# Expert weights of a routed SwGLU layer: 32 KB per partition in five joined slots from the third expert on, instead of 16 KB in ten

## The chip, the cores and the metric

The kernel runs on one core of a Trainium2 chip (trn2), as one program with one launch. Time is device time in microseconds (us), from the first to the last instruction of an execution with what lies around it; a run's time is one execution, and medians are over several. All numbers are float32.

## What is computed

One layer of a diffusion backbone: 512 latent tokens and 256 context tokens of width 1024. The first sub-layer (a state-space branch and a latent-attention branch, gated and merged) is not touched by the change. The second is a set of 16 experts, each of which picks its 64 best tokens. Cut to what matters:

```python
def expert_choice_ffn(h, w_router, w_gate, w_up, w_down):
    aff = jax.nn.softmax((h @ w_router).astype(jnp.float32), axis=-1)
    gate, idx = lax.top_k(aff.transpose(0, 2, 1), cap)              # cap = 64 of 512 tokens
    xs = h[bidx, idx]
    hid = jax.nn.silu(jnp.einsum('becd,edf->becf', xs, w_gate)) * jnp.einsum('becd,edf->becf', xs, w_up)
    ys = jnp.einsum('becf,efd->becd', hid, w_down) * gate[..., None].astype(h.dtype)
    return jnp.zeros_like(h).at[bidx, idx].add(ys)
```

The weights of one expert are gate and up, 1024 x 2816 each, and down, 2816 x 1024: 33 MiB in float32, 528 MiB for the 16. Every one of them is used once.

## The kernel before

The first sub-layer, the router and the top-64 selection come first. Then the experts run one after the other, in a Python loop that is unrolled (`for e in range(NE)`, L1487). An expert's hidden width of 2816 is cut into six chunks: five of 512 columns and one of 256. Each chunk goes through two steps.

- `hidden` (L1501 to 1515; called H below): for 8 slices of the input width, one matmul with the gate weights and one with the up weights (L1505, tile `pgu`), then SiLU on ScalarE (L1507, tile `hd`), the product on VectorE (L94), four transposes on TensorE (L1512, `phT`) and a copy back to SBUF on ScalarE (L1514, `hT`).
- `down` (L1517 to 1521; called D): two matmuls for each 128 hidden columns, added up over the expert in one PSUM tile (L1520, `pdn`).

After the last chunk one VectorE instruction weights the result (`ye`), and GpSimd adds its rows into the output by an indirect DMA (L1539). `gather(e + 1)`, which builds the next expert's input (`pxg`, `pxt`, `pinf` on TensorE), is written ahead of chunk 3. A scheduler sets the order on each engine; on SyncE's queue (SP), which issues all weight loads, it is the order of the code.

The weights are stored in blocks that are ready for the loads: `w_e_gu` has 11 blocks of 128 x 4096 for an expert (two for each chunk of 512, holding the first and the second four slices of the input width; one for the last chunk), `w_e_down` has 5 blocks of 128 x 4096, and `w_e_down_end` one of 128 x 2048. So an expert has 16 loads of 2 MiB, with 16 KB for each partition, and one of 1 MiB. `ring` (L1442) puts each 2 MiB load into the next of ten slots in the fixed order `RING`; the slots are pools of one buffer each, and a load waits until the readers of the slot's last contents are done. At most eight loads are under way at a time: each has one of eight completion semaphores in turn, and SP waits for the load that had it last. The ten slots lie where the first sub-layer's tiles lay, so the first loads are issued as that memory comes free.

The last expert is written with each D behind the next chunk's H. All others are written H, D, H, D.

Of the kernel before, what the change touches and what calls it, by code (L numbers as in the profile page):

```python
# [18 lines left out]
D = 1024  # L19
# [7 lines left out]
NE = 16  # L27
# [21 lines left out]
NPK = _off  # L49
NTRI = 193  # L50
NR, NL = 13, 7

RING = ("L0", "R1", "R3", "R5", "R2", "R4", "R0", "L1", "L2", "L3")

# [2 lines left out]
def hybrid_block(ctx: ExitStack, tc: tile.TileContext, A, out, dbg=None, stop=99):  # L57
    nc = tc.nc
    V, S, G, T = nc.vector, nc.scalar, nc.gpsimd, nc.tensor
    dma, dmr = nc.sync.dma_start, G.dma_start  # L60

    def pool(name, st=ctx, **kw):
        return st.enter_context(tc.tile_pool(name=name, bufs=kw.pop("bufs", 1), reuse_waits="tile", **kw))
# [6 lines left out]
    cur = {}  # L70
# [13 lines left out]
    def pg(name, shape=(128, 512)):  # L84
        return psg.tile(list(shape), F32, name=name, tag="pg")
# [94 lines left out]
    rows = {}  # L180
# [35 lines left out]
    for j in range(4):  # L216
        t = tl("xx", f"X{j}", [NCH, 2, D])
# [416 lines left out]
    for k in range(8):  # L634
# [4 lines left out]
        h = tl("gt", "hxf", [128, 512])  # L639
# [222 lines left out]
    for gb in range(4):  # L862
# [16 lines left out]
        t, y = s5_T(gb, yb)  # L879
# [85 lines left out]
    t = tl("gt", "krt2", [128, 6, 32])  # L965
# [346 lines left out]
    for b in range(8):  # L1312
        if b % 4 == 0:
            wmo = wload("w_mla_o", 0, 4, 128 * b, 512)
        if b % 2 == 0:
            c = 256 * ((b % 4) // 2)
            wms = wsplit(wmo[:, :, c:c + 256], 4, 256)
        c = 128 * (b % 2)
# [11 lines left out]
    for n in range(2):  # L1330
        for kh in range(2):
            w = wload("w_out", 4 * kh, 4, 512 * n, 512)
# [101 lines left out]
    chunks = [(512 * i, 512) for i in range(5)] + [(2560, 256)]  # L1434
    nring = [0]
    ph2.close()
    for n in ("R0", "R1", "R2", "R3", "R4", "R5", "small"):
        cur[n] = pool(n, side="right")
    for n in ("L0", "L1", "L2", "L3"):
        cur[n] = pool(n)  # L1440

    def ring(name, src, rn):  # L1442

        w = src.shape[1]
        r = "small"
        if w > 2048:
            r = RING[nring[0] % len(RING)]
            nring[0] += 1
        t = tl(r, name, [128, w])
        dma(t, src)  # L1450
        return [t[:, w // rn * i:w // rn * (i + 1)] for i in range(rn)]

    def gather(e):

# [31 lines left out]
    nxt_ = gather(0)  # L1486
    for e in range(NE):  # L1487
        xe, ge, sidx = nxt_
        wgu, wd, wds = [A[n][e] for n in ("w_e_gu", "w_e_down", "w_e_down_end")]
        po = pg("pdn")  # L1490

        def load_gu(f0, fn):
            if fn == 256:
                return ring("wgu", wgu[10], 16)
            a, b = [ring("wgu", wgu[f0 // 256 + i], 8) for i in range(2)]
            return a[:4] + b[:4] + a[4:] + b[4:]

        def load_d(f0, fn):
            return ring("wd", wds, 2) if fn == 256 else ring("wd", wd[f0 // 512], 4)

        def hidden(wt_, fn):  # L1501
            p = pw("pgu", (128, 512))
            for k in range(8):
                for j in range(2):
                    T.matmul(p[64 * j:64 * j + 64, :fn], xe[:, k, :], wt_[8 * j + k], start=(k == 0), stop=(k == 7))  # L1505
            hd = l2("hd", [64, 512])
            S.activation(hd[:, :fn], p[0:64, :fn], AF.Silu)  # L1507
            mul(hd[:, :fn], hd[:, :fn], p[64:128, :fn])
            ph = pa("phT", (128, 4, 64))
            n = fn // 128  # L1510
            for b in range(n):
                T.transpose(ph[:, b, :], hd[:, 128 * b:128 * b + 128], ident[0:64, 0:64])  # L1512
            hT = l2("hT", [128, 4, 64])
            S.copy(hT[:, :n], ph[:, :n])  # L1514
            return hT

        def down(hT, td, f0):  # L1517
            for b, w in enumerate(td):
                for h in range(2):
                    T.matmul(po[64 * h:64 * h + 64, :], hT[:, b, :], w[:, 512 * h:512 * h + 512],  # L1520
                             start=(f0 == 0 and b == 0), stop=(f0 + 128 * b == FF - 128))

        if e < NE - 1:
            for f0, fn in chunks:
                if f0 == 1536:
                    nxt_ = gather(e + 1)
                wt_, td = load_gu(f0, fn), load_d(f0, fn)
                down(hidden(wt_, fn), td, f0)
        else:
            hts = []  # L1530
            for i, (f0, fn) in enumerate(chunks):
                hts.append(hidden(load_gu(f0, fn), fn))
                if i:
                    f1, fm = chunks[i - 1]
                    down(hts[i - 1], load_d(f1, fm), f1)
            down(hts[-1], load_d(f0, fn), f0)
        ye = l2("ye", [128, 512])
        stt(ye, po, ge, g2bc, ALU.mult, ALU.mult)
        G.indirect_dma_start(out=o2, out_offset=bass.IndirectOffsetOnAxis(ap=sidx, axis=0),  # L1539
                             in_=ye, in_offset=None, compute_op=ALU.add)  # L1540
# [3 lines left out]
def layout(inputs):  # L1544
    import numpy as np

    a = {k: np.asarray(v) for k, v in inputs.items()}
    f32 = np.float32
    pk = np.zeros((128, NPK), f32)

    def put(n, v):
        o, w = PK[n]
        pk[:v.shape[0], o:o + w] = v

    def cols(v):
        return np.ascontiguousarray(v.reshape(-1, 128).T)

    def ssm(v):
        rest = v.shape[3:]
        v = v.reshape((2, 4, 2, 4, 64) + rest)  # L1560
        v = np.moveaxis(v, (2, 4, 1, 0, 3), (0, 1, 2, 3, 4))
        return np.ascontiguousarray(v).reshape((128, 32) + rest)

    put("c", cols(a["c"][0]))
    put("cc", cols(a["c_ctx"]))
    put("bada", cols(a["b_ada"][0]))
    put("g1n", cols(a["norm1_g"][0]))
    put("g2n", cols(a["norm2_g"][0]))
    put("qag", cols(a["q_a_g"][0]))
    put("kvag", cols(a["kv_a_g"][0]))  # L1570
    put("bglu", cols(a["b_glu"][0]))
    put("sd", a["ssm_d"][0].reshape(4, 2, 4, 16).transpose(2, 1, 3, 0).reshape(128, 4))
    put("lre", ssm(a["ssm_lam_re"][0]))
    put("lim", ssm(a["ssm_lam_im"][0]))
    put("ldt", ssm(np.broadcast_to(a["ssm_log_dt"][0][:, :, None], (2, 32, 64))))
    put("gq", a["q_norm_g"][0][:, None])
    put("gk", a["k_norm_g"][0][:, None])
    sw = np.arange(32).reshape(2, 2, 8)[:, ::-1].reshape(-1)
    gq, gk = a["q_norm_g"][0][64:], a["k_norm_g"][0][64:]
    put("grope", np.broadcast_to(np.concatenate([gq, gq[sw], gk, gk[sw]]), (128, 128)))  # L1580
    tok = (8 * np.arange(64)[None, None, :] + 2 * np.arange(4)[:, None, None] + np.arange(2)[None, :, None]).reshape(4, 128)
    inv = f32(10000.0) ** (-np.arange(8, dtype=f32) / f32(8))
    pos = np.stack([tok // 64, tok % 64], -1).astype(f32)
    ang = (pos[..., None] * inv).astype(np.float64)
    cs, sn = np.cos(ang), np.sin(ang)
    cs = np.stack([cs, cs], 3).reshape(4, 128, 32)
    sn = np.stack([-sn, sn], 3).reshape(4, 128, 32)
    put("rcos", cs.transpose(1, 0, 2).reshape(128, 128).astype(f32))
    put("rsin", sn.transpose(1, 0, 2).reshape(128, 128).astype(f32))
    put("tok", tok.T.astype(f32))  # L1590
    put("ident", np.eye(128, dtype=f32))
    put("hmask", np.tile(np.eye(16, dtype=f32), (8, 1)))
    put("stack", np.tile(np.eye(32, dtype=f32), (4, 1)))

    def ct(v):
        return ssm(np.swapaxes(v, -1, -2))

    tri = np.zeros((128, NTRI), f32)
    tri[:, :128] = np.triu(np.ones((128, 128), f32))
    tri[:, 128:192] = np.arange(1, 65)  # L1600
    tri[64:, 192] = 1
    r = {"pk": pk, "tri": tri,
         "ssm_b": np.ascontiguousarray(np.stack([ssm(a["ssm_b_re"][0]), ssm(a["ssm_b_im"][0])], 1)),
         "ssm_c": np.ascontiguousarray(np.stack([ct(a["ssm_c_re"][0]), ct(a["ssm_c_im"][0])], 1)),
         "x": a["x"][0], "ctx": a["ctx"][0]}
    for n in ("w_ada", "b_ada", "w_in", "w_qb", "w_kvb", "w_mla_o", "w_glu", "w_ssm_o", "w_out", "w_router"):
        r[n] = a[n][0]

    w = [a[n][0].reshape(NE, 8, 128, FF).transpose(0, 2, 1, 3) for n in ("w_e_gate", "w_e_up")]
    b = np.empty((NE, 11, 128, 2, 2048), f32)  # L1610
    for i in range(2):
        m = w[i][..., :2560].reshape(NE, 128, 2, 4, 5, 512).transpose(0, 4, 2, 1, 3, 5)
        b[:, :10, :, i] = m.reshape(NE, 10, 128, 2048)
        b[:, 10, :, i] = w[i][..., 2560:].reshape(NE, 128, 2048)
    r["w_e_gu"] = b.reshape(NE, 11, 128, 4096)
    w = a["w_e_down"][0]
    r["w_e_down"] = w[:, :2560].reshape(NE, 5, 4, 128, D).transpose(0, 1, 3, 2, 4).reshape(NE, 5, 128, 4096)
    r["w_e_down_end"] = w[:, 2560:].reshape(NE, 2, 128, D).transpose(0, 2, 1, 3).reshape(NE, 128, 2048)
    return {k: np.ascontiguousarray(v) for k, v in r.items()}


# [17 lines left out]
```

## Time and profile before

| What | us |
| --- | --- |
| median of 3 runs | 1923.01 (1919.36 to 1924.98) |
| the profiled execution | 1919.85 |
| its span, from first to last instruction | 1918.1 |
| TensorE busy with matmuls in it | 1633.8 (85%) |
| VectorE / ScalarE / GpSimd busy in it | 531.5 / 320.7 / 209.9 |

The span falls into two stretches. In the first 620 us, the first sub-layer, the engines share the work and the DMA engines are partly idle. From there to the end TensorE and the DMA engines are both nearly always at work, and the other engines rest. Busy TensorE time is the time in which some matmul was under way, and says nothing of how well it was used.

### The profile page before, as it was taken

To read this page: it belongs to the slowest core of one execution; us is meant where nothing else is said; L and a number is where in the kernel's file an instruction comes from. 1 tells how busy PE (TensorE), PEld (TensorE's weight loads), DVE (VectorE), ACT (ScalarE), POOL (GpSimd) and SP (SyncE) were. 2 spreads that over 40 slices of the span, in tenths; PEclk is the share of its full clock that TensorE was granted. 3 is DMA by queue.
4 is the path that set the end of the run, shared out by engine and by line. 5 is a ranking of instruction groups with operands and counts; after the bars stand their busy time and mean duration, and the time that the engine had idled before them with its cause. 6 is when DMAs were issued, how large, how long until landed. Compare 5 with 4: busy or idle time off the path is not lost.

```text
span 1918.1 us, 20921 instructions
## 1 busy us (share of the span) xinstructions
PE 1633.8 (85%) x8660; PEld 791.5 (41%) x8660; DVE 531.5 (28%) x1180; ACT 320.7 (17%) x593; POOL 209.9 (11%) x218
## 2 busy tenths in 40 slices
PE   3798999999995988888888888888888788888886
PEld 2586778755573333333333333323223232332322
DVE  7877665675745101011000100001000010100000
ACT  3422225364421000000000000000000000000000
POOL 3667200231110000000000000000000000000000
PEclk8899999999997999999999999999999999999999
DMA  9243353525539899999999999999999999999996
GB/s 316 57 141 111 105 189 133 170 97 201 157 90 401 363 422 426 422 427 420 422 427 422 421 426 422 426 423 423 425 421 427 421 427 421 420 428 421 427 422 281
DMA packets 108654, 642.56 MB, mean 335 GB/s; under 512 B 10256, under 2 KB 45072, under 8 KB 73232
## 3 DMA queue, kind: packets, MB, share of 16 engines
q1 hardware_dynamic: 105040, 631.79, 81.2%
q0 software_dynamic: 2880, 7.34, 1.7%
q10 hardware_dynamic: 640, 2.10, 0.3%
q8 instruction: 68, 1.11, 0.2%
q14 instruction: 26, 0.21, 0.0%
HBM read 623.93 MB, written 17.27 MB: 334 GB/s over the span
## 4 chain that ended last, share of the span: by engine, by line
PE 43%; DMA 36%; DVE 8%; issue 5%; ACT 3%; POOL 2%; POOLq 0%; ACTq 0%; SPq 0%; DVEq 0%
DMA wgu<-in_w_e_gu 18%; PE pgu L1505 14%; DMA wd<-in_w_e_down 10%; PE pdn L1520 8%; DMA wd<-in_w_e_down_end 6%; PE pxg L1462 2%; PE po L1263 1%; DVE hd L94 1%; PE px L122 1%; PE px L124 1%; PE px L123 1%; ACT hd L1507 1%; PE ada L191 1%; PE phT L1512 1%; PE py L801 1%
## 5 line engine op out<-in xcount | busy, mean ns | idle before, releaser
L1505 PE MATMUL pgu<-wgu,xe 128*64 128x512 f32 (+1 forms) x3072 | 644.9, 559 | 27.5 <-DMA wgu<-in_w_e_gu 26.0
L1505 PEld LDWEIGHTS pgu<-wgu,xe 128*64 128x64 f32 x3072 | 219.9, 137 | 426.5 <-issue 351.1
L1520 PE MATMUL pdn<-wd,hT 128*64 128x512 f32 x1408 | 357.5, 645 | 34.5 <-ACT hT L1514 34.5
L94 DVE TENSOR_TENSOR hd<-hd,pgu 64x512 f32<-64x512 f32 x96 | 61.9, 645 | 994.3 <-ACT hd L1507 994.3
L1507 ACT ACTIVATE hd<-pgu 64x512 f32<-64x512 f32 x96 | 53.3, 556 | 951.5 <-PE pgu L1505 951.5
L1520 PEld LDWEIGHTS pdn<-wd,hT 128*64 128x64 f32 x1408 | 110.9, 146 | 214.2 <-issue 163.6
L1539 POOL DMA_INDIRECT out<-ye,sidx x16 | 24.9, 1556 | 1340.7 <-DVE ye L112 1340.7
L1512 PE MATMUL phT<-pk,hd 64*128 64x64 f32 x352 | 42.1, 236 | 126.7 <-DVE hd L94 126.7
L1512 PEld LDWEIGHTS phT<-pk,hd 64*128 64x128 f32 x352 | 29.0, 138 | 204.3 <-DVE hd L94 204.3
L122 PE MATMUL px<-hx,ws 128*128 128x512 f32 x200 | 81.1, 406 | 6.3 <-ACT hx L637 6.3
L123 PE MATMUL px<-hx,ws 128*128 128x512 f32 x200 | 80.1, 400 | 3.5 <-DVE hx L94 3.4
L124 PE MATMUL px<-hx,ws 128*128 128x512 f32 x200 | 79.5, 398 | 1.4 <-DVE ws L94 1.4
L1462 PE MATMUL pxg<-xm,oh 128*64 128x512 f32 x256 | 75.3, 609 | 0.6 <-DVE oh L94 0.6
L1514 ACT COPY hT<-phT 128x256 f32<-128x256 f32 x96 | 34.1, 355 | 119.2 <-PE phT L1512 119.2
L122 PEld LDWEIGHTS px<-hx,ws 128*128 128x128 f32 x200 | 38.4, 192 | 15.3 <-ACT hx L637 6.4
L123 PEld LDWEIGHTS px<-hx,ws 128*128 128x128 f32 x200 | 38.1, 190 | 14.7 <-DVE hx L94 7.6
L124 PEld LDWEIGHTS px<-hx,ws 128*128 128x128 f32 x200 | 38.2, 191 | 10.2 <-DVE ws L94 2.5
L1466 DVE COPY xg<-pxg 128x256 f32<-128x256 f32 x16 | 6.8, 424 | 127.1 <-ACT xg L1465 127.1
L1462 PEld LDWEIGHTS pxg<-xm,oh 128*64 128x64 f32 x256 | 30.6, 140 | 21.1 <-issue 19.4
L1233 DVE TENSOR_REDUCE mx<-ps 128x1 f32<-128x768 f32 x32 | 30.5, 954 | 27.7 <-PE ps L124 25.0
L354 PE MATMUL xT<-pk,X 96*128 96x96 f32 x64 | 11.5, 348 | 29.1 <-DMA craw<-in_ssm_c 18.7
L191 PE MATMUL ada<-wada,scv 128*32 128x512 f32 x192 | 34.1, 675 | 0.0
(471 smaller groups left out, 1724.5 us busy)
## 6 DMA issues: line engine op xcount, KB each, us to landing
wgu<-in_w_e_gu SPq DMA_DIRECT2D x176, 2048.0 KB, 37.9
wd<-in_w_e_down SPq DMA_DIRECT2D x80, 2048.0 KB, 37.9
wada<-in_w_ada SPq DMA_DIRECT2D x16, 1024.0 KB, 7.7
wd<-in_w_e_down_end SPq DMA_DIRECT2D x16, 1024.0 KB, 36.8
wada<-in_w_ada SPq DMA_DIRECT2D x16, 512.0 KB, 10.6
win_g<-in_w_in SPq DMA_DIRECT2D x16, 512.0 KB, 4.3
gs<-gt SPq DMA_DIRECT2D x16, 256.0 KB, 2.0
g<-gs SPq DMA_DIRECT2D x16, 256.0 KB, 3.2
```

The lines of the kernel that those rows point to most:

```text
L94: (e or V).tensor_tensor(o, a, b, op=op)
L122: T.matmul(o, a[0], b[0], start=first, stop=False)
L123: T.matmul(o, a[0], b[1], start=False, stop=False)
L124: T.matmul(o, a[1], b[0], start=False, stop=last)
L191: T.matmul(p[32 * q:32 * q + 32, :], scv[:, k].rearrange("p s n -> p (s n)"), w[q], start=(k == 0), stop=(k == 7))
L1233: V.tensor_reduce(mx, p[:, 0:768], AX.X, ALU.max, negate=True)
L1462: T.matmul(px[64 * h:64 * h + 64, :], oh[:, t], xms[t][:, 512 * h:512 * h + 512], start=(t == 0), stop=(t == 3))
L1505: T.matmul(p[64 * j:64 * j + 64, :fn], xe[:, k, :], wt_[8 * j + k], start=(k == 0), stop=(k == 7))
L1507: S.activation(hd[:, :fn], p[0:64, :fn], AF.Silu)
L1512: T.transpose(ph[:, b, :], hd[:, 128 * b:128 * b + 128], ident[0:64, 0:64])
L1514: S.copy(hT[:, :n], ph[:, :n])
L1520: T.matmul(po[64 * h:64 * h + 64, :], hT[:, b, :], w[:, 512 * h:512 * h + 512], start=(f0 == 0 and b == 0), stop=(f0 + 128 * b == FF - 128))
```

## The change

The stored form of the weights changes. Each expert has 8 blocks of 128 x 8192 (32 KB for each partition, `w_e_big`) and the 128 x 2048 end. Five blocks hold a whole chunk of gate and up (`GU`: blocks 0, 1, 3, 4, 6), two hold two chunks of down each (blocks 2 and 5), and the last holds the gate and up of the small chunk beside the fifth chunk of down (`DN`).

For the first two experts the loads are still halves of 16 KB (`half`), into the ten slots. At the third (`NE16 = 2`) the pools of the ten slots are closed and five pools of twice the size are opened in the same memory: `RING32`, where R23 covers R2 and R3, and so on. From there one load fetches a block; the very last block of the last expert is fetched in two. The steps of an expert are now in the order H0 H1 D0 D1 H2 H3 D2 D3, gather, H4 D4 H5 D5, and in the last expert H4 H5 D4 D5.

```diff
+NE16 = 2
+
+GU = (0, 1, 3, 4, 6)
+DN = ((2, 0), (2, 1), (5, 0), (5, 1), (7, 1))
+RING32 = ("R23", "R45", "L23", "L01", "R01")
...
-    def ring(name, src, rn):
+    def ring(name, src, parts=1):
         w = src.shape[1]
         r = "small"
         if w > 2048:
-            r = RING[nring[0] % len(RING)]
+            order = RING if w == 4096 else RING32
+            r = order[nring[0] % len(order)]
             nring[0] += 1
         t = tl(r, name, [128, w])
-        dma(t, src)
-        return [t[:, w // rn * i:w // rn * (i + 1)] for i in range(rn)]
+        for i in range(parts):
+            c = slice(w // parts * i, w // parts * (i + 1))
+            dma(t[:, c], src[:, c])
+        return t
...
+        if e == NE16:
+            ph3.close()
+            for n in ("R01", "R23", "R45", "small"):
+                cur[n] = pool(n, side="right")
+            for n in ("L01", "L23"):
+                cur[n] = pool(n)
+            nring[0] = 0
+
+        have = {}
+
+        def half(b, h):
+            if e >= NE16:
+                if b not in have:
+                    have[b] = ring("wb", big[b], 2 if b == 7 and e == NE - 1 else 1)
+                return have[b], 4096 * h
+            return ring("wb", big[b][:, 4096 * h:4096 * h + 4096]), 0
...
-        if e < NE - 1:
-            for f0, fn in chunks:
-                if f0 == 1536:
-                    nxt_ = gather(e + 1)
-                wt_, td = load_gu(f0, fn), load_d(f0, fn)
-                down(hidden(wt_, fn), td, f0)
-        else:
-            hts = []
-            for i, (f0, fn) in enumerate(chunks):
-                hts.append(hidden(load_gu(f0, fn), fn))
-                if i:
-                    f1, fm = chunks[i - 1]
-                    down(hts[i - 1], load_d(f1, fm), f1)
-            down(hts[-1], load_d(f0, fn), f0)
+        hts = {}
+        last = e == NE - 1
+        for st in (("H0", "H1", "D0", "D1", "H2", "H3", "D2", "D3", "H4", "H5", "D4", "D5") if last else
+                   ("H0", "H1", "D0", "D1", "H2", "H3", "D2", "D3", "G", "H4", "D4", "H5", "D5")):
+            if st == "G":
+                nxt_ = gather(e + 1)
+                continue
+            c = int(st[1])
+            f0, fn = chunks[c]
+            if st[0] == "H":
+                hts[c] = hidden(load_gu(f0, fn), fn)
+            else:
+                down(hts.pop(c), load_d(f0, fn), f0)
```

Three places in the built programs. First, SP's queue where the second expert ends and the third begins; before (`wgu` and `wd` are the tiles of gate-and-up and of down; the numbers tell buffers apart):

```order
L1450 DMA wgu_5955<-in_w_e_gu 128x4096
L1450 DMA wgu_5957<-in_w_e_gu 128x4096
L1450 DMA wd_5959<-in_w_e_down 128x4096
L1450 DMA wgu_5996<-in_w_e_gu 128x4096
L1450 DMA wd_5998<-in_w_e_down_end 128x2048
L1450 DMA wgu_6033<-in_w_e_gu 128x4096
L1450 DMA wgu_6035<-in_w_e_gu 128x4096
L1450 DMA wd_6037<-in_w_e_down 128x4096
```

And SP's queue at the same place now (`wb` is a block, or a half of one):

```order
L1460 DMA wb_5955<-in_w_e_big 128x4096
L1460 DMA wb_5957<-in_w_e_big 128x4096
L1460 DMA wb_5986<-in_w_e_big 128x4096
L1460 DMA wb_5996<-in_w_e_big 128x4096
L1460 DMA wd_6023<-in_w_e_end 128x2048
L1460 DMA wb_6062<-in_w_e_big 128x8192
L1460 DMA wb_6091<-in_w_e_big 128x8192
L1460 DMA wb_6120<-in_w_e_big 128x8192
```

The third expert's first chunk (`wb_6062`) is one load of 4 MiB where it was two of 2 MiB (`wgu_6033`, `wgu_6035`), and the down weights (`wb_6120`) come after two chunks of gate and up.

Second, TensorE's row at the start of the first expert, before:

```order
L1505 MATMUL pgu_5471<-wgu_5465,xe_5442 64x512 x8
L1505 MATMUL pgu_5471<-wgu_5467,xe_5442 64x512 x8
L1505 MATMUL pgu_5512<-wgu_5506,xe_5442 64x512 x7
L1512 MATMUL phT_5491<-pk_69,hd_5488 128x64 x4
L1505 MATMUL pgu_5512<-wgu_5506,xe_5442 64x512
L1505 MATMUL pgu_5512<-wgu_5508,xe_5442 64x512
L1520 MATMUL pdn_5464<-wd_5469,hT_5496 64x512 x8
L1505 MATMUL pgu_5512<-wgu_5508,xe_5442 64x512 x7
```

And TensorE at the same place now:

```order
L1544 MATMUL pgu_5469<-wb_5465,xe_5442 64x512 x8
L1544 MATMUL pgu_5469<-wb_5467,xe_5442 64x512 x8
L1544 MATMUL pgu_5500<-wb_5496,xe_5442 64x512 x7
L1551 MATMUL phT_5489<-pk_69,hd_5486 128x64 x4
L1544 MATMUL pgu_5500<-wb_5496,xe_5442 64x512
L1544 MATMUL pgu_5500<-wb_5498,xe_5442 64x512 x8
L1559 MATMUL pdn_5464<-wb_5527,hT_5494 64x512 x3
```

The third slot to be read to its end was that of the first down weights (`wd_5469`); now it is that of the second chunk's first half (`wb_5496`), which is done right behind the transposes.

Third, TensorE's row at the end of the last expert, before:

```order
L1505 MATMUL pgu_9883<-wgu_9879,xe_9584 64x512 x8
L1505 MATMUL pgu_9883<-wgu_9881,xe_9584 64x512 x8
L1512 MATMUL phT_9903<-pk_69,hd_9900 128x64 x4
L1520 MATMUL pdn_9724<-wd_9910,hT_9867 64x512 x8
L1505 MATMUL pgu_9922<-wgu_9920,xe_9584 64x256 x16
L1512 MATMUL phT_9942<-pk_69,hd_9939 128x64 x2
L1520 MATMUL pdn_9724<-wd_9947,hT_9908 64x512 x8
L1520 MATMUL pdn_9724<-wd_9957,hT_9945 64x512 x4
```

And TensorE at the same place now:

```order
L1544 MATMUL pgu_9700<-wb_9698,xe_9450 64x512 x16
L1544 MATMUL pgu_9730<-wb_9727,xe_9450 64x256 x7
L1551 MATMUL phT_9720<-pk_69,hd_9717 128x64 x4
L1544 MATMUL pgu_9730<-wb_9727,xe_9450 64x256 x9
L1551 MATMUL phT_9750<-pk_69,hd_9747 128x64 x2
L1559 MATMUL pdn_9545<-wb_9727,hT_9725 64x512 x8
L1559 MATMUL pdn_9545<-wd_9763,hT_9753 64x512 x4
```

The fourth D (`wd_9910`) has moved ahead of this piece, H4 reads one block (`wb_9698`) where it read two, and seven matmuls of H5 stand between H4 and its transposes. (Each matmul of the program counts twice in the trace: an H of 512 columns is 16 here and x32 in a row of the trace.)

## Rows read from the trace of the kernel before

**Rows 1.** The page's DMA lines over 40 slices of the span.

```profile
DMA  9243353525539899999999999999999999999996
GB/s 316 57 141 111 105 189 133 170 97 201 157 90 401 363 422 426 422 427 420 422 427 422 421 426 422 426 423 423 425 421 427 421 427 421 420 428 421 427 422 281
```

**Rows 2.** The page's DMA issues: count, size of one, median us to landing.

```profile
wgu<-in_w_e_gu SPq DMA_DIRECT2D x176, 2048.0 KB, 37.9
```

**Rows 3.** Window of the experts: us, busy us (count) by engine, clock, DMA share, GB/s.

```profile
650.00:1890.00 1240.00, 1052.88 (x5170) 386.19 (x5168) 110.44 (x302) 89.46 (x199) 23.35 (x15) 0.98 1.01 424
```

**Rows 4.** SP's waits from 1200 to 1500 us: us in total, times, longest.

```profile
SPq L1450 <- DMA wgu<-in_w_e_gu: 183.3, 40, 5.6
SPq L1450 <- DMA wd<-in_w_e_down: 83.5, 18, 5.9
...
SPq L1450 <- PE pdn L1520: 1.6, 6, 0.3
```

**Rows 5.** SP's issues in the steady stretch: start, us, what, how many.

```profile
1242.96 2.81 SPq L1450 DMA_DIRECT2D wgu<-in_w_e_gu  x2
1250.34 0.33 SPq L1450 DMA_DIRECT2D wd<-in_w_e_down  x1
1255.25 5.48 SPq L1450 DMA_DIRECT2D wgu<-in_w_e_gu  x2
...
1325.07 2.82 SPq L1450 DMA_DIRECT2D wgu<-in_w_e_gu  x2
1332.45 0.33 SPq L1450 DMA_DIRECT2D wd<-in_w_e_down  x1
```

**Rows 6.** Windows at the start of the experts, columns as in rows 3.

```profile
625.00:630.00 5.00, 4.27 (x20) 1.49 (x22) 1.28 (x7) 0.00 (x0) 0.00 (x0) 1.00 0.15 62
...
640.00:645.00 5.00, 5.00 (x26) 1.58 (x22) 0.00 (x0) 0.46 (x1) 0.00 (x0) 1.00 0.76 242
645.00:650.00 5.00, 4.46 (x24) 1.66 (x24) 0.69 (x1) 0.50 (x2) 0.00 (x0) 1.00 1.05 449
```

**Rows 7.** SP's issues at the start of the experts, columns as in rows 5.

```profile
608.08 21.67 SPq L1450 DMA_DIRECT2D wgu<-in_w_e_gu  x2
632.85 0.33 SPq L1450 DMA_DIRECT2D wd<-in_w_e_down  x1
641.12 1.27 SPq L1450 DMA_DIRECT2D wgu<-in_w_e_gu  x2
```

**Rows 8.** The chain that ended last, TensorE's first two experts: start, us, what.

```profile
625.73 10.51 PE pgu L1505 x46
...
662.31 2.69 PE pxg L1462 x13
...
680.24 6.89 PE pgu L1505 x32
...
700.23 6.89 PE pgu L1505 x32
...
740.93 2.69 PE pxg L1462 x13
```

**Rows 9.** Waits from 640 us on: D for the copy of its input; us, times, longest.

```profile
PE pdn L1520 <- ACT hT L1514: 34.5, 73, 0.5
```

**Rows 10.** Timeline at the end; in brackets the idle time before, and its releaser.

```profile
1889.65 5.35 PE L1505 MATMUL pgu<-wgu,xe 128*64 128x512 f32 x16 [2.65 <-DMA wgu<-in_w_e_gu]
...
1896.81 3.65 PE L1520 MATMUL pdn<-wd,hT 128*64 128x512 f32 x16
...
1900.29 3.62 PE L1505 MATMUL pgu<-wgu,xe 128*64 128x256 f32 x32
...
1905.11 5.37 PE L1520 MATMUL pdn<-wd,hT 128*64 128x512 f32 x24
...
1910.53 0.75 DVE L112 SCALAR_TENSOR_TENSOR ye<-pdn,ge,g2bc 128x512 f32<-128x512 f32 x1 [5.74 <-PE pdn L1520]
```

**Rows 11.** Window at the end, columns as in rows 3.

```profile
1890.00:1895.00 5.00, 5.00 (x16) 1.27 (x12) 0.00 (x0) 0.00 (x0) 0.00 (x0) 0.66 1.02 433
```

## What the change was predicted to do

> **What bounds the kernel now.** I read the DMA lines over the 40 slices first. From the thirteenth slice on the DMA share is 9 in every slice but the last, and the rate stays between 420 and 428 GB/s once the fourteenth is past [rows 1]. One window over the 1240 us from 650 to 1890 gives a DMA share of 1.01 at 424 GB/s; TensorE is busy 1052.88 us of it at a granted clock of 0.98, so it has slack [rows 3]. The chain that ended last runs over TensorE in the first experts [rows 8], but that is a question of who hands over to whom: the DMA engines move as much there as later [rows 1]. SP's own waits say which end is late in the steady stretch: from 1200 to 1500 us it waited 183.3 us and 83.5 us for earlier loads to land, and 1.6 us for D's readers of a slot [rows 4]. A load lands 37.9 us after its issue [rows 2], nearly eight times the 4.9 us that one takes (below). So the queue is full, and the experts take the time that 528 MiB take on the DMA engines, plus a head before the stream is full and a tail behind it. A faster TensorE gives nothing there; only the time of a MiB, gaps in the stream, and the tail count.
>
> **The price of a MiB.** In the steady stretch SP issues when the load of eight places earlier has landed, so its issues tick off landings [rows 5]. A row that covers two issues ends with the second, and an issue takes 0.33 us: the second of the first row begins at 1242.96 + 2.81 - 0.33 = 1245.44. From 1245.44 to 1250.34 is 4.90 us, from there to 1255.25 is 4.91: 2 MiB, 4.905 us, 427.6 GB/s. From 1242.96 to 1245.44 is 2.48 us: the 1 MiB end of an expert, with rows of 8 KB, 422.8 GB/s; a turn later it is 1325.07 + 2.82 - 0.33 - 1325.07 = 2.49. Two loads of 1 MiB with half the row length thus take 2 x 2.48 = 4.96, 0.055 us more than one of 2 MiB (0.05 to 0.08 over these readings). That is what a load costs for being a load, with the eight rows that each of the 16 engines moves in it, in a full queue.
>
> The change makes one load of 4 MiB out of two of 2 MiB, with rows twice as long and as many of them: 8 times in each of 14 experts, less one for the last block, which is fetched in two: 111. If a step from 16 to 32 KB saves what the step from 8 to 16 KB shows, 111 x 0.055 = 6.1 us, and with the larger readings up to 111 x 0.08 = 8.9. No row has a 32 KB row, so the bounds are wider: nothing saved if such rows move as two pieces of 16 KB, and on the other side a loss (rivals). I take 6.4 us, near the reading, since it is the nearest row: same queue, same stretch, one doubling away.
>
> The Trainium skill speaks of this price too (DMA: Bandwidth & Descriptors, "Anatomy of one DMA"): a fixed part of about 2.0 us for each DMA issued from GpSimd, most of it the wait for the write to be confirmed, plus the bytes at 436 GB/s. If that fixed part stood in the stream, 111 fewer loads would give 222 us, and the time would be 1701 us. A load of 1 MiB in 2.48 us does not bear it out: by that rule it alone would take an estimated 4.4 us. I give that case less than 1 in 100.
>
> **The start.** The ten slots are full when TensorE begins the experts at 625.73 [rows 8], and the stream stands still until it frees the first slot: 62 GB/s in the window from 625 to 630 [rows 6], and the second load of the row at 608.08 is issued as late as 608.08 + 21.67 - 0.33 = 629.42 [rows 7]. None of this changes, since H0 reads the same two halves first. The second slot comes free at 632.85, but the third held the down weights of chunk 0, whose D ends at 641.12 [rows 7]. In between the stream ran dry: 242 and 449 GB/s in the two windows from 640 to 650 [rows 6], a mean of 345.5 against 424, so 18.5% of 10 us, 1.9 us lost. Now the third slot holds the first half of H1. TensorE has done 23 of the 24 matmuls up to its end by 625.73 + 10.51 = 636.24 [rows 8], and the last follows the transposes, at about 638. The two loads before it keep the stream until about 629.4 + 1 + 2 x 4.9 = 640. So the gap closes: 1.9 us gained (bounds 0 and 1.9).
>
> **The change of slots.** At the third expert a load of 32 KB needs two old slots. Its first two blocks wait for the two halves of the second expert's H3, the third for the end of its H4. Could the stream run dry there? Loads up to the second block are 2 x 16.5 + 4 = 37 units of 2 MiB; 10 are in at 629.4, and 27 take 27 x 4.905 = 132.4 us, with 1 us to start and about 1.2 us for the first expert's output rows (a turn of 82.11 us, from 1250.34 to 1332.45 [rows 5], less 16.5 x 4.905). The stream has work until 764. TensorE: H3 and H4 now follow H and not D's copy, and a D waited 0.47 us for that copy (34.5 us in 73 times [rows 9]), which falls away four times in an expert, 1.9 us. The first expert took 700.23 - 625.73 = 74.5 us, so the second now starts at about 698.3. A turn from gather to gather is 740.93 - 662.31 = 78.6 [rows 8], 76.7 with the new order; from the end of H4 to the next expert before was 700.23 - 680.24 - 6.89 = 13.1. H4 ends at about 698.3 + 76.7 - 13.1 = 761.9, and the load begins to move about 1 us later. Cover: 1 us. I put this at 0 and keep 5 us for the range. Afterwards four loads of 4 MiB stand in the queue whenever one is read, 39 us, the depth of before; the order H0 H1 D0 D1 asks for no more of TensorE than before, so nothing waits there. SP's waits for readers take the place of those for landings, before a queue that is as deep; behind them on SP stand only later loads.
>
> **The tail.** Before, the last half of H4 starts at 1889.65, when its load has landed, and VectorE's last instruction at 1910.53 [rows 10]: 20.9 us, all TensorE, with D3, H5, D4 and D5 behind it. Now H4 waits for the whole 4 MiB. Behind it in the stream are 5 MiB instead of 7, so it lands 4.9 us later in an equal stream. Then: H4 whole 6.9 us [rows 8]; 7 of 16 matmuls of H5 beside SiLU and product, and the transposes, 1.8, the gap between the half H4 and D3; 9/16 of H5's 3.6 us, 2.0; its SiLU, product and transposes, 1.2, the gap from 1900.29 + 3.62 to 1905.11; D4 and D5, 5.4 [rows 10]; 17.3 us. D2 and D3, 2 x 3.65 us, fit into the 9.8 us between their landing and that of H4's block. So 4.9 + 17.3 - 20.9 = 1.3 us longer. The half H4 took 5.35 us behind a wait of 2.65 us, in a window whose granted clock was 0.66, between the levels of 1.2 and 2.4 GHz [rows 10, 11]; a full clock would have needed 3.5. If the whole H4 meets the same, 1.7 us more. I take 1.3, with 0 and 3.4 as bounds.
>
> **The sum**: - 6.4 - 1.9 + 0 + 1.3 = - 7.0 us. The profiled execution of 1919.85 us would become 1912.8; it lies 3.2 us below the median of the three runs, near their lowest. Against the median of 1923.01 I predict 1916.0.
>
> **Rivals.** First, the length of a row is worth nothing: the rows are moved in pieces of 16 KB, or 0.055 us is how two loads share the engines and not a price. For it: one step of size is all that the trace shows, and 0.055 is close to how finely landings can be read. Against it: the 2.48 us recurs within 0.01. Then - 1.9 + 1.3 = - 0.6 us, 1922.4.
>
> Second, the change of slots starves the stream. TensorE's pace decides: at the old pace H4 of the second expert ends at 700.23 + 78.6 - 13.1 = 765.7, and the stream stands from 764 to 766.7, 2.7 us; a slower gather could make it 5. Then 1918.7 to 1921, say 1919.
>
> Third, and slower: long rows move worse. The first two experts now read 16 KB out of rows that lie 32 KB apart, and later ones 32 KB at a time. If the doubling lost as much rate as the last one gained, 422.8 instead of 427.6 GB/s, a load of 4 MiB would take 9.92 us instead of 9.81: 111 x 0.11 = 12.2 us, and with - 1.9 + 1.3 the time is 1934.6. It decides from a landing interval of about 9.87 us on. For it: the 1 MiB and 2 MiB loads show that the row length has an effect at all. Against it: at 427.6 GB/s the doubling from 8 to 16 KB helped. The Trainium skill has a rule on this side (DMA: Bandwidth & Descriptors, "Latency and other measured facts"): copies of 128 rows of 16 KB between HBM tensors slow down when the rows lie a large power of two apart, slightly at 512 KB and by half at 4 MB. No row here has a pitch above 16 KB in the weights, so the trace neither shows nor denies it at 32 KB.
>
> **How the numbers follow.** Forecast 0.60, no worth in long rows 0.22, starved stream 0.08, worse rows 0.10. About 0.3%, 5.8 us, is what a measurement of this kernel can tell from no change. Of the forecast's 0.60, with gains from about 3 to 11 us, 0.52 lie above that bound; its rest, the first rival and the second are the same: 0.38; the third is slower: 0.10. The range: the forecast's largest gain is 8.9 + 1.9 = 10.8, with 3 us for the scatter of medians 1909; upward it takes in the first rival and 3 us of scatter, 1926. Outside are the third rival and a little on either side.
>
> **What would show it.** In the changed trace, landing intervals of 4 MiB loads near 9.75 us in the steady stretch say that the price is right; 9.81, the first rival; above 9.87, the third. A window from 640 to 650 us near 424 GB/s shows the start, and a dip between 760 and 770 us the second rival. The last H4 should start 15 to 19 us before VectorE's last instruction. I am wrong if the stream shows gaps in the steady stretch, for then five slots are too few, and that is in no part of this sum.

## The result and the profile after

The changed kernel takes 1910.15 us (median of 4 runs, 1907.65 to 1910.76), beside 1921.37 of the kernel before (4 runs): a ratio of 0.9937, with an interval from 0.9918 to 0.9956. That is faster by 0.63%. The forecast was 1916.0, and the range from 1909 to 1926 holds the result, about 1 us from its lower end. The profiled execution took 1909.72 us, 10.1 less than the one of before, with a span of 1907.9. The forecast for that difference was 7.0, so the sum had the sign right and was 3 us short. One of the twelve runs of two_loads (an experiment below) took 2252.69 us at a granted clock of 0.729, where the other eleven had 0.967 to 0.974, and is left out of its figures.

The page of the changed kernel begins like that of the kernel before [rows 1]. The DMA share is 9 from the fifteenth slice to the last but one (the prediction said from the thirteenth, but the fourteenth reads 8 in both), and the rate is a little higher: most slices read 423 to 433 GB/s where they read 420 to 428.

```profile
DMA  9153354425539899999999999999999999999996
GB/s 319 56 147 103 108 177 146 172 89 182 164 107 390 374 421 433 416 431 424 425 429 427 430 426 426 427 425 432 424 427 426 425 432 424 431 424 423 432 425 267
```

**The rate.** The clearest view of it is what the weights' queue moved in one stretch that is equal for both kernels, 800 us from 1050 to 1850: packets, MB, and their share of the 16 engines' time. Below them is a row of DMA issues: what, count, KB each, and the median us from issue to landing. First the kernel before, then the changed one.

```profile
q1 hardware_dynamic: 23770, 335.74, 98.9%
...
out<-ye,sidx POOLq DMA_INDIRECT x10, 11.4
```

```profile
q1 hardware_dynamic: 12702, 338.56, 98.6%
...
wb<-in_w_e_big SPq DMA_DIRECT2D x79, 4096.0 KB, 34.3
...
out<-ye,sidx POOLq DMA_INDIRECT x10, 16.3
```

The engines were as full as before and moved 2.82 MB more. An expert is 33 MiB, 34.60 MB. At 335.74 MB in 800 us it takes 82.45 us, at 338.56 MB it takes 81.76: 0.69 us less for each expert, with eight merges in it, so 0.086 us for each merge of two loads of 2 MiB into one of 4 MiB. The window of the steady stretch, to be held against [rows 3], says it more coarsely: 427 GB/s where it was 424.

```profile
650.00:1880.00 1230.00, 1057.36 (x5162) 380.56 (x5160) 112.49 (x302) 89.30 (x199) 23.34 (x15) 0.95 1.01 427
```

**The start and the change of slots.** The two windows that read 242 and 449 GB/s [rows 6] now read 416 and 423, and those where the old slots are joined, from 760 to 770, read 413 and 400 (columns as in rows 3).

```profile
640.00:645.00 5.00, 4.46 (x26) 1.51 (x24) 0.69 (x1) 0.96 (x2) 0.00 (x0) 1.00 0.99 416
645.00:650.00 5.00, 5.00 (x26) 1.68 (x24) 0.00 (x0) 0.00 (x0) 0.00 (x0) 1.00 0.99 423
...
760.00:765.00 5.00, 3.51 (x20) 1.07 (x16) 0.69 (x1) 0.62 (x2) 0.00 (x0) 1.00 1.04 413
765.00:770.00 5.00, 4.61 (x28) 1.97 (x30) 0.00 (x0) 0.34 (x1) 0.00 (x0) 1.00 0.95 400
```

At the start the mean rose from 345.5 to 419.5, which is (419.5 - 345.5) / 424 x 10 = 1.7 us gained. At the joining the mean is 406.5 against a mean rate before of 424, which would be 0.4 us lost. That is no empty queue: the DMA share of the two windows is 1.04 and 0.95. Nor is the loss sure, since windows this short scatter by as much: cut_rows (below), whose slots are joined in the same way, reads 406 and 436 there, and two_loads 429 twice.

**SP's waits** have turned over, as the prediction said they would: all of them from 1200 to 1500 us are for readers of a slot, where they were for landings [rows 4].

```profile
SPq L1460 <- PE pgu L1544: 187.3, 22, 10.7
SPq L1460 <- PE pdn L1559: 101.4, 8, 14.1
```

One of the proofs that the prediction named is gone with this: SP's issues no longer tick off landings, so landing intervals of 4 MiB can't be read from them. The bytes in 800 us take their place.

**A wait that nobody foresaw** stands in the waits from 640 to 1890 us (engine and what it did, what it waited for, us in total, times, longest).

```profile
PE phT L1551 <- DVE hd L100: 151.7, 93, 4.2
ACT hd L1546 <- DMA out<-ye,sidx: 119.6, 14, 9.4
...
PE pgu L1544 <- DMA wb<-in_w_e_big: 1.0, 1, 1.0
```

`ye`, the weighted result of an expert, and `hd` come from one pool of four buffers. In the new order two H stand at the head of an expert, and the SiLU of the second needs the buffer from which GpSimd's indirect DMA is still reading the last expert's `ye`. It happens between every two experts but one (14 times). ScalarE then stands 8 to 9 us, but most of that it would have waited for TensorE in any case: in the place below the matmuls of the second H begin at 1189.88 and take 7.09 us, and the SiLU comes 1.5 us behind their end. TensorE's transposes behind it wait up to 4.2 us. One such place in the timeline:

```profile
1189.88 7.09 PE L1544 MATMUL pgu<-wb,xe 128*64 128x512 f32 x32
...
1198.44 0.59 ACT L1546 ACTIVATE hd<-pgu 64x512 f32<-64x512 f32 x1 [8.03 <-DMA out<-ye,sidx]
...
1199.81 0.46 PE L1551 MATMUL phT<-pk,hd 64*128 64x64 f32 x4 [2.84 <-DVE hd L100]
```

So the chain that ended last now runs through `out<-ye` (12% of it by the page). Whether that costs anything is a question for an experiment (own_ye).

**The tail.** In the timeline at the end, to be held against [rows 10], the last H4 starts at 1882.41 behind its landing, and VectorE's last instruction at 1900.58: 18.2 us, where the prediction had worked out 17.3 and the kernel before took 20.9.

```profile
1882.41 8.81 PE L1544 MATMUL pgu<-wb,xe 128*64 128x512 f32 x46 [0.99 <-DMA wb<-in_w_e_big]
...
1891.54 2.37 PE L1544 MATMUL pgu<-wb,xe 128*64 128x256 f32 x18
...
1895.16 3.65 PE L1559 MATMUL pdn<-wb,hT 128*64 128x512 f32 x16
...
1900.58 0.75 DVE L118 SCALAR_TENSOR_TENSOR ye<-pdn,ge,g2bc 128x512 f32<-128x512 f32 x1 [5.74 <-PE pdn L1559]
```

### The profile page after: what moved, and what is told of

It reads as the page before. It is cut to its first block, busy times and chain, and to the rows that moved or that the text cites. A ratio compares the mean times of both kernels' runs of the same rounds, so it can differ in the third digit from the quotient of the medians.

```text
span 1907.9 us, 20694 instructions
## 1 busy us (share of the span) xinstructions
PE 1639.4 (86%) x8660; PEld 786.7 (41%) x8660; DVE 532.2 (28%) x1180; ACT 320.3 (17%) x593; POOL 208.6 (11%) x218
## 4 chain that ended last, share of the span: by engine, by line
PE 62%; DMA 13%; DVE 9%; issue 5%; ACT 4%; POOL 2%; ACTq 0%; POOLq 0%; SPq 0%; DVEq 0%
PE pgu L1544 21%; PE pdn L1559 17%; DMA out<-ye,sidx 12%; PE pxg L1476 4%; DVE hd L100 3%; ACT hd L1546 2%; PE phT L1551 2%; PE po L1269 2%; PE px L128 1%; PE px L130 1%; PE px L129 1%; PE ada L197 1%; PE py L807 1%; DVE z L784 1%; PE ppt L1257 1%
## 5 line engine op out<-in xcount | busy, mean ns | idle before, releaser
L1544 PE MATMUL pgu<-wb,xe 128*64 128x512 f32 (+1 forms) x3072 | 625.3, 558 | 2.2 <-DVE xe L100 1.2
L1544 PEld LDWEIGHTS pgu<-wb,xe 128*64 128x64 f32 x3072 | 216.4, 137 | 370.8 <-issue 349.1
L1559 PE MATMUL pdn<-wb,hT 128*64 128x512 f32 x1280 | 343.0, 676 | 6.9 <-ACT hT L1553 6.9
L1559 PEld LDWEIGHTS pdn<-wb,hT 128*64 128x64 f32 x1280 | 107.2, 155 | 206.6 <-issue 195.8
L1476 PE MATMUL pxg<-xm,oh 128*64 128x512 f32 x256 | 81.9, 700 | 5.3 <-DVE oh L100 5.3
L130 PEld LDWEIGHTS px<-hx,ws 128*128 128x128 f32 x200 | 38.8, 194 | 10.7 <-DVE ws L100 2.8
L1476 PEld LDWEIGHTS pxg<-xm,oh 128*64 128x64 f32 x256 | 24.3, 153 | 39.5 <-issue 27.7
L1559 PE MATMUL pdn<-wd,hT 128*64 128x512 f32 x128 | 30.9, 604 | 6.1 <-ACT hT L1553 6.1
## 6 DMA issues: line engine op xcount, KB each, us to landing
wd<-in_w_e_end SPq DMA_DIRECT2D x16, 1024.0 KB, 30.4
```

What stands on the lines that cost most here:

```text
L130: T.matmul(o, a[1], b[0], start=False, stop=last)
L1476: T.matmul(px[64 * h:64 * h + 64, :], oh[:, t], xms[t][:, 512 * h:512 * h + 512], start=(t == 0), stop=(t == 3))
```

## The experiments

Two theories of the gain were to be told apart. By the first, it is the length of a row: a piece of 32 KB costs less than two of 16 KB. By its rival, it is the number of loads: each load costs something for being one. A third question was how much the order of the steps, the joined slots and the tail add or take. All diffs are against the changed kernel. Ratios are to the kernel before on the same chip: again, two_loads, cut_rows and halves_all ran on one (kernel before 1920.74 us, 32 runs), four_loads, join_second, own_ye and tail on another (1923.04 us, 11 runs).

### The changed kernel again

> The changed kernel itself, beside the experiments on the same chip. Both theories expect about 1910 us, 11 us under the kernel before, since nothing is edited; it sets the level for the other three.

It took 1912.04 us (9 runs), a ratio of 0.9952 (0.9936 to 0.9967). It is the measure for the others of its chip.

### Joined slots, but two loads for a block

```diff
-                    have[b] = ring("wb", big[b], 2 if b == 7 and e == NE - 1 else 1)
+                    have[b] = ring("wb", big[b], 2)
```

> The changed kernel, but every 32 KB block is fetched in two loads of 16 KB rows into its joined slot; slots, step order and start are those of the changed kernel. If the gain is the price of a piece of 16 KB (about 0.085 us for each 4 MiB, 111 times), some 9 us come back: about 1919 us, with 424 GB/s in the steady stretch. If the gain comes from the joined slots and the new step order, it stays at about 1910 us and 427 GB/s.

1918.19 us (11 runs), a ratio of 0.9985 (0.9970 to 0.9999). The rows of the 800 us:

```profile
q1 hardware_dynamic: 23776, 335.77, 98.9%
```

Of the 0.0048 by which the changed kernel's ratio lies below 1, 0.0033 are gone (6.15 us by the medians), and the bytes in 800 us are those of the kernel before. Some 9 us were expected back. The missing part is found at the end: with the last blocks in smaller loads, VectorE's last instruction starts 4.0 us behind the end of the weight stream, where it is 6.4 in the changed kernel (table further down). The joined slots, the stored form and the order of the steps all stand here as in the changed kernel. So the higher rate comes from the merging, and whether it is the load or the row is left for the next experiment. Beside that, rows of 16 KB that lie 32 KB apart move as fast as rows that lie 16 KB apart: 335.77 against 335.74 MB.

### One load for a block, but in rows of 16 KB

The two halves of a row are stored apart, so that one load of 4 MiB has 256 rows of 16 KB.

```diff
+        if two and parts == 1:
+            dma(t.rearrange("p (h c) -> p h c", h=2), src.rearrange("h p c -> p h c"))
+            return t
...
-    r["w_e_big"] = b
+    r["w_e_big"] = b.reshape(NE, 8, 128, 2, 4096).transpose(0, 1, 3, 2, 4)
```

> The changed kernel with as many loads as it has, one for each block, but the two halves of a row are stored apart, so that each load of 4 MiB moves 256 pieces of 16 KB instead of 128 of 32 KB. If the price is the piece's, about 1918 us (nearly all of 9 us comes back). If it is the load's (its completion, its issue), about 1910 to 1911 us.

1919.59 us (12 runs), a ratio of 0.9995 (0.9982 to 1.0007): within the scatter the whole gain is gone, with as few loads as in the changed kernel. The rows of the 800 us, and the page's count for the whole execution, then the page's count of the changed kernel and of the kernel before:

```profile
q1 hardware_dynamic: 22546, 335.91, 98.8%
...
wb<-in_w_e_big SPq DMA_DIRECT2D x78, 4096.0 KB, 42.5
...
q1 hardware_dynamic: 103264, 631.78, 81.1%
```

```profile
q1 hardware_dynamic: 89056, 631.78, 80.8%
```

```profile
q1 hardware_dynamic: 105040, 631.79, 81.2%
```

The counts tell what a merge takes away. Against before, this kernel has 1776 packets less, 111 x 16: one for each engine and merge. The changed kernel has 15984 less, 111 x 144: those 16, and 128 rows more. The first 16 are worth at most the difference between 335.91 and 335.74 MB, 0.04 us an expert; the 128 are worth the rest of 0.69. It is the row, and the rival falls. A row saved is 0.086 us x 16 engines / 128 = about 10.7 ns on one engine. The trace also has a record of each single row, and its times say the same: by the median from 1050 to 1850 us, a row of 8 KB takes 313 ns (four_loads), one of 16 KB 614 (before) and one of 32 KB 1216 (changed), so that two rows take 12 ns more than one of twice the length, at both steps.

### Rows of 8 KB

```diff
-                    have[b] = ring("wb", big[b], 2 if b == 7 and e == NE - 1 else 1)
+                    have[b] = ring("wb", big[b], 4)
```

> The changed kernel with every 32 KB block fetched in four loads of 8 KB rows. The cut rows cost about 0.68 us an expert against whole ones, for 64 pieces more on each engine, or 10.6 ns a piece. If that is a price of each piece whatever its length, 8 KB rows add twice as many pieces again: 128 x 10.6 ns x 14 = 19 us on top of the kernel with two loads, about 1937 us, and a turn of an expert of 83.8 us. If 16 KB was a threshold above which rows run better, about 1918 us, as with two loads.

1938.52 us (4 runs), a ratio of 1.0080 (1.0056 to 1.0105). The rows of the 800 us:

```profile
q1 hardware_dynamic: 45385, 330.49, 99.6%
...
out<-ye,sidx POOLq DMA_INDIRECT x10, 9.0
```

At 330.49 MB an expert takes 83.76 us, 1.31 more than with 16 KB, for 16 splits: 0.082 us for a split. The price is nearly the same at both doublings. Nothing in these rows has to do with a threshold between 16 and 32 KB, and this also measures anew the step that the prediction read as 0.055.

### The new order alone

```diff
-NE16 = 2
+NE16 = 16
```

All experts are loaded in halves of 16 KB into the ten slots; the slots are never joined.

> The new step order alone: all 16 experts in loads of 16 KB rows into the ten slots, which are never joined. If long rows carry the gain, only the gap at the start closes, 1.4 to 1.9 us: about 1919.5 us. If the step order carries it, about 1911 us.

1916.69 us (12 runs), a ratio of 0.9985 (0.9972 to 0.9998). The windows at the start, and then the rows of the 800 us:

```profile
640.00:645.00 5.00, 4.46 (x24) 1.52 (x22) 0.69 (x1) 0.96 (x2) 0.00 (x0) 1.00 1.00 423
645.00:650.00 5.00, 5.00 (x26) 1.62 (x24) 0.00 (x0) 0.00 (x0) 0.00 (x0) 1.00 1.01 429
```

```profile
q1 hardware_dynamic: 23782, 335.83, 98.9%
```

The gap at the start is closed by the order of the steps alone, and the steady rate is that of before. The ratio is worth 2.9 us (0.4 to 5.4), in line with 1.9 us at the start, (426 - 345.5) / 424 x 10. That it is equal to the ratio of two_loads, in which the slots are joined, says that the joining costs less than these runs can tell.

### Joining the slots one expert sooner

```diff
-NE16 = 2
+NE16 = 1
```

> The slots are joined one expert earlier, so the second expert's first block waits for R2 and R3, the last of which the first expert's D4 reads. The stream has work until about 629.4 + 1 + 6.5 x 4.9 = 662 us, and D4 of the first expert ends at about 693 us in the changed kernel's trace. If a dry stream is paid in full, the DMA engines stand about 31 us and the time is about 1941 us, less 0.7 us for one more expert in long rows. If TensorE's slack swallows part of it, less than 1930 us.

1941.39 us (4 runs), a ratio of 1.0090 (1.0065 to 1.0115). This is the prediction's second rival, made to happen. From 660 us on the stream runs dry, and it stands until after 690, while TensorE works through its ten slots (columns as in rows 3):

```profile
650.00:660.00 10.00, 8.59 (x42) 2.85 (x40) 0.69 (x1) 0.96 (x2) 0.00 (x0) 1.00 1.00 428
660.00:670.00 10.00, 8.21 (x42) 3.11 (x39) 1.18 (x3) 0.96 (x2) 0.00 (x0) 1.00 0.33 139
670.00:680.00 10.00, 10.00 (x63) 5.46 (x61) 1.54 (x7) 0.37 (x1) 0.00 (x0) 1.00 0.01 2
680.00:690.00 10.00, 8.12 (x40) 2.72 (x38) 1.40 (x6) 0.96 (x2) 0.00 (x0) 0.98 0.00 0
690.00:700.00 10.00, 8.66 (x50) 3.77 (x48) 0.42 (x1) 0.64 (x2) 0.00 (x0) 0.85 0.55 210
...
1050.00:1850.00 800.00, 682.45 (x3274) 241.79 (x3272) 72.24 (x197) 56.73 (x126) 13.91 (x9) 0.93 1.01 427
```

Against 428 GB/s, (289 + 426 + 428 + 218) / 428 x 10 = 31.8 us are missing from 660 to 700. The kernel is 28.3 us slower than own_ye of the same chip, which has the changed kernel's time. Nearly all of the gap is thus paid, though the rate behind it is the higher 427. In the two profiled executions the stream is 30.4 us longer than the changed kernel's (table further down), and with 0.7 us for one more expert in long rows that is 31.1 of the 31.8.

### A buffer of its own for the result

```diff
-        ye = l2("ye", [128, 512])
+        ye = pk[:, 0:512]
```

`ye` goes to columns of the constants' tile that nobody reads any more, so the SiLU waits for no indirect DMA.

> The changed kernel, but the weighted output of an expert is written to columns of the constant tile that nothing reads any more, so that no SiLU waits for the indirect DMA to have read it. In the changed kernel that wait is 119.6 us over 14 experts. If the stream alone sets the time, no change: about 1911 us. If TensorE, which hardly waits for weights any more, sets it, up to 1.4 us an expert come back: about 1892 us.

1913.06 us (6 runs), a ratio of 0.9949 (0.9930 to 0.9968): the changed kernel's. The waits from 640 to 1880 us:

```profile
PE phT L1551 <- DVE hd L100: 125.4, 93, 1.5
...
PE pgu L1544 <- DMA wb<-in_w_e_big: 19.8, 18, 3.0
...
PE pdn L1559 <- DMA wb<-in_w_e_big: 10.9, 7, 1.8
```

The unforeseen wait is gone: no row for `out` stands there, and the transposes wait 125.4 us, not 151.7. In its place TensorE waits 30.7 us for weights, where it waited 1.0. The new wait had only filled slack. It had 12% of the chain that ended last and was worth nothing.

### The tail drawn together

On top of own_ye, the last expert runs H4, H5 and D4 ahead of D2 and D3, and its last three blocks are each fetched in two halves. The hidden values of H2 and H3 lie in spare columns of the constants' tile in the meantime.

```diff
-                    have[b] = ring("wb", big[b], 2 if b == 7 and e == NE - 1 else 1)
+                    have[b] = ring("wb", big[b], 2 if b > 4 and e == NE - 1 else 1)
...
-        for st in (("H0", "H1", "D0", "D1", "H2", "H3", "D2", "D3", "H4", "H5", "D4", "D5") if last else
+        for st in (("H0", "H1", "D0", "D1", "H2", "H3", "H4", "H5", "D4", "D2", "D3", "D5") if last else
```

> As own_ye, and the last expert in the order H0 H1 D0 D1 H2 H3 H4 H5 D4 D2 D3 D5, its blocks for H4, H5, D4, D2 and D3 fetched in two loads each. The last load then feeds only D5, and the one before it D3. In the changed kernel VectorE's last instruction comes about 7 us behind the end of the weight stream. If the work behind the last bytes sets the tail, it shrinks to about 4 us: about 1908 us. If TensorE's backlog sets it, no change, about 1911 us.

1910.88 us (6 runs), a ratio of 0.9932 (0.9911 to 0.9953). TensorE's end, where one wait for a load is left, of 0.23 us:

```profile
1893.83 3.65 PE L1559 MATMUL pdn<-wb,pk 128*64 128x512 f32 x16 [0.23 <-DMA wb<-in_w_e_big]
1897.32 1.89 PE L1559 MATMUL pdn<-wd,hT 128*64 128x512 f32 x8
```

By the medians this is 2.2 us below own_ye, but the intervals of the two lie over each other. The end behaves as meant: VectorE's last instruction starts 3.4 us behind the end of the weight stream, where it was 6.4 in own_ye. But the profiled execution also began its experts 1.8 us later than that of own_ye (626.66 against 624.87 us), in the first sub-layer, which no edit touches. That the new end makes the kernel faster is not shown.

## Why the prediction came out right, and where its sum was short

**What bounds the kernel**: right. A higher rate of the stream came through, a dry stream is paid nearly in full (join_second), and a wait of TensorE in the steady stretch is worth nothing (own_ye).

**The price of a MiB**: the mechanism was right, the term mis-sized. The prediction took 111 x 0.055 = 6.1, rounded up to 6.4, and kept 8.9 as its upper reading. Measured are 111 x 0.086 = 9.5 us, a little above even that. The step that failed is the reading itself, not the carrying over from one doubling to the next: in four_loads the doubling from which it was read costs 0.082. The term came from 2 x 2.48 - 4.905, and an error of 0.01 in one landing becomes 0.02 in the difference. The second landing interval of 2.49 that the prediction quotes would alone have given 0.075. Such a small difference wants a view that adds up many loads, as the bytes in 800 us do. The name that the prediction gave to the price, "what a load costs for being a load, with the eight rows that each of the 16 engines moves in it", left open which of the two it is. It is the rows: cut_rows has the changed kernel's loads and the old time.

**The start**: right. 1.7 us by the windows, for a forecast of 1.9, and halves_all shows that it belongs to the order of the steps.

**The change of slots**: right, at 0.4 us or less for a forecast of 0 with up to 5 kept. The stream did not run dry there, though the cover was put at 1 us only. join_second shows what stood behind it.

**The tail**: a little too small. H4's start came 7.2 us sooner than before [rows 10]. By the trace's records of single rows, the last row of weights ended at 1894.21 us, and at 1906.37 before, 12.2 us sooner. So in an equal stream H4 landed 4.9 us later, as forecast (4.2 if the stream's end is taken 1 MB earlier). The piece behind it took 18.2 us, not 17.3, with 2.37 us where 2.0 was put for the rest of H5, and the remainder spread over H4 and its transposes. Together that is 4.9 + 18.2 - 20.9 = 2.2 (or 1.5), for a forecast of 1.3. The feared 1.7 us for a low clock did not come: the windows of H4 were granted 1.00, the upper level of 2.4 GHz, where the one before had 0.66 [rows 11].

```profile
1880.00:1885.00 5.00, 4.01 (x20) 1.17 (x18) 0.00 (x0) 0.00 (x0) 0.00 (x0) 1.00 0.96 408
1885.00:1890.00 5.00, 5.00 (x30) 1.89 (x28) 0.00 (x0) 0.46 (x1) 0.00 (x0) 1.00 0.64 264
```

**The sum by its measured terms.** The same records give each profiled execution two lengths: the stream's, from TensorE's first expert matmul to the end of the last weight row, and the tail's, from there to the start of VectorE's last instruction.

| Kernel | stream, us | tail, us |
| --- | --- | --- |
| before | 1280.6 | 4.2 |
| changed | 1269.0 | 6.4 |
| two_loads | 1278.3 | 4.0 |
| cut_rows | 1278.3 | 6.3 |
| halves_all | 1278.7 | 4.0 |
| four_loads | 1297.4 | 3.2 |
| join_second | 1299.4 | 7.4 |
| own_ye | 1269.0 | 6.4 |
| tail | 1269.2 | 3.4 |

The longer rows are worth 9.3 us (cut_rows to changed; 9.5 by the bytes), and the new order with the joined slots 2.3 (before to cut_rows), of which halves_all has 1.9 without joining. The tail costs 2.2. That is - 9.3 - 2.3 + 2.2 = - 9.4 us, where the forecast had - 6.4 - 1.9 + 1.3 = - 7.0: the price of the rows was too small by about 3 us, and the tail, with the other sign, by up to 1, so a part of the error was cancelled by luck. Another 0.5 us came from outside the sum, since TensorE began the experts sooner (625.19 us, not 625.73 [rows 8]), in the first sub-layer that the change does not touch: - 9.9, beside the 10.1 between the two profiled executions. TensorE's first row of the experts in the timeline after:

```profile
625.19 10.51 PE L1544 MATMUL pgu<-wb,xe 128*64 128x512 f32 x46 [1.18 <-DVE xe L100]
```

**The rivals.** That the length of a row is worth nothing falls with four_loads and the bytes of the changed kernel, and that long rows move worse falls with the same. On the pitch, the Trainium skill's rule on large powers of two (DMA: Bandwidth & Descriptors, "Latency and other measured facts") names 512 KB and more; at the 32 KB of two_loads no loss shows. The wait that the prediction did not see at all, that of a SiLU for an indirect DMA, cost nothing only because TensorE had slack. "The order H0 H1 D0 D1 asks for no more of TensorE than before, so nothing waits there" was wrong as a statement on waits, and right on time.

## What to carry to other kernels

Where the DMA queue is always full, ask what one row (one contiguous piece) costs and make rows longer; fewer loads of the same rows give nothing. Read a price that small from the bytes moved in a long equal stretch, not from a few landing intervals. When slots are made larger, check that the stream stays fed at the place where the old slots are joined, for a dry stream is paid nearly in full, while a new wait on an engine with slack may stand first on the chain and be worth nothing.

## What the runs showed of the hardware

An indirect DMA takes longer to land the longer the rows are that move beside it. `out<-ye,sidx` (128 rows of 2 KB, eight on each engine) landed 9.0 us after its issue beside rows of 8 KB, 11.4 beside 16 KB and 16.3 beside 32 KB. cut_rows, with loads of 4 MiB in rows of 16 KB, has 11.9, so it goes by the row and not by the load:

```profile
out<-ye,sidx POOLq DMA_INDIRECT x10, 11.9
```

Eight rows of weights on one engine are 2.48 us at 8 KB, 4.905 at 16 KB [rows 5], and about 9.7 at 32 KB (2 x 4.905 less 0.086). Less these, the landing is 6.5, 6.5 and 6.6 us. So each of the eight rows of the indirect DMA seems to wait for one row of the weights. The records of single rows show that it does. The rows and completions of one indirect DMA begin over 3.8, 6.3 and 11.1 us beside rows of 8, 16 and 32 KB (medians). A row of the indirect DMA takes 176 ns itself, and eight times it and one row of the weights (313, 614 or 1216 ns) is 3.9, 6.3 and 11.1 us.

The Trainium skill has each DMA engine take turns between its queues by whole packets, typically of 9 to 17 descriptors (DMA: Bandwidth & Descriptors, "Queues, rings and completion order"). The turns measured here are shorter than such a packet: one row each.

The price of longer rows is thus that a buffer which such a DMA reads is held longer. The wait of the SiLU for `ye` comes from it: two_loads, cut_rows and halves_all have the same order of steps with rows of 16 KB, and their waits from 640 to 1880 us have no such row.
